# First up-projection chunk: a place of its own for the last row block, reordered transfers, some weight sums on GpSimd, and gathers listed ahead of the unit's own share

## The chip, the cores and the metric

The kernel runs on one core of a Trainium2 chip. Its time is the device time of one execution in microseconds (us). The engines are PE (TensorE), DVE (VectorE), ACT (ScalarE), POOL (GpSimd) and SP (SyncE, which here only issues transfers). The median of 3 runs before the change is 2326.56 us (2325.76 to 2328.48).

## The reference

One decoder layer over a prompt of 2048 tokens and a sample of 8 x 8 tokens, D_MODEL 1024, D_FF 4096, all in float32:

```python
h = rms_norm(x, g_mix_pre)
# projection, sliding-window attention, gated linear attention
mix = einsum('bte,ed->btd', concat(attn, gla), w_out)
x = x + rms_norm(mix, g_mix_post)

h = rms_norm(x, g_ffn_pre)
u = relu(einsum('btd,df->btf', h, w_up))
f = einsum('btf,fd->btd', u * u, w_down)
x = x + rms_norm(f, g_ffn_post)
```

The change touches the seam between the two halves (the residual of the last row blocks, and the start of the feed-forward part) and the loop over w_down.

## The kernel before

**Products.** Each float32 operand is split into a high and a low fp32r part: ACT copies (high), DVE subtracts (low), and PE multiplies three times (high high, high low, low high); `split_by` and `split_copy` are these two instructions. Both feed-forward products use a scheme of seven products in place of eight on 2 x 2 blocks (Strassen's, in Winograd's form), so that sums of blocks of h, of w_up, of w_down and of the activations are made beforehand. Products are numbered p = 1 to 7; 0, 8 and 9 stand for the sample's part, which is computed plainly.

**Row blocks.** The prompt has 16 blocks of 128 rows (0 to 15), the sample is block 16. `B_ORDER` takes them in the order 0, 4, 1, 5, 2, 6, 3, 7, 16, 8, 12, 9, 13, 10, 14, 11, 15. `residual(i, ...)` is a generator with five yields: (1) squares of the out product on ACT, mean and power (DVE, then POOL's `pow`); (2) scaling by `gpost` into x1; (3) x added, a store of x1 for the end of the layer, square and power again; (4) scaling by `gpre`; (5) eight transposes on PE into PSUM and two ACT copies into `ht`; after that four DVE subtractions and a store of `ht` to `h_d`, for the second block of a pair. `run(res, n)` advances it by n steps. The last block, 15, is advanced step by step inside the first chunk of the up projection.

**Up projection.** `up(g, before)` works on chunk g of 256 columns of w_up: g = 0 to 15 with the first half of the prompt (and the sample), 16 to 31 with the second half. PE runs the products in the order `UP_FIRST` = (1, 0, 2, 8, 5, 7, 9, 6, 3, 4) in chunk 0 and `UP_ORDER` = (1, 5, 7, 0, 6, 3, 8, 2, 9, 4) in the others; after each product, the branch for this p issues what belongs to it. PSUM banks: X (p = 1, 2), Z (5, 3), Y (6), V (7, 4). The tile `s` of a chunk has seven rows of 512; `s[:, 1]` is a copy of X, `s[:, 3]` one of Z. Products p = 3 and p = 2 add to Z and X, so they wait for these copies. `H[p]` is operand p of h: 1 and 2 are made from the transposes, the others are fetched from `h_d` by `fetch_h` and split by `split_h`. Weights: `load_up(g)` fetches the chunk into `raws[g]`, `split_up` splits it, `sums_13` and `sums_24` make the sums (two DVE instructions each), and `split_sums` splits them; the sums of g + 1 are made during chunk g. `load_down` and `sum_down` do the same for w_down, which is stored in `t_d`. At the end of a chunk the generator `end` finishes rows 1 and 2 of `s` in the next chunk, and the tile is stored to `s_d`.

**Places.** `s` of odd chunks lies in pool `st1`, which also holds `ht`; `s` of even chunks in `st0`. Operands 3, 5, 7, 6, 4 and `st0` take the place of w_out's parts, so a transfer into them waits until the last out products have read those. Blocks 11 and 15 get x in the place "h0" of `hs_pool`, one after the other.

**Order.** `te`, `ac`, `dv` and `sy` are `InOrder` wrappers of PE, ACT, DVE and SP: what is issued through them keeps the order of the program. What is issued through `nc.sync`, `nc.vector` or `nc.gpsimd` is put in place by the scheduler. An engine takes its instructions in order, and so does SP: a transfer that waits keeps the later ones waiting.

**Down projection.** 7 passes p (`DOWN_ORDER` = (6, 1, 5, 7, 2, 3, 4)) for each half of the prompt, each of 16 units. A unit n is four banks of three products (`down_products`), with two more into the bank `sam` in passes 1, 5, 2, 3 of the first half. `down_fetch(n + 3)` and `down_split(n + 1)` run ahead. When a pass ends (fc == NFC - 1), its banks are handed as generators to the list `todo`, from which each unit takes work worth 1.4 (`room`): `gather` adds or copies a bank into the result (0.7 each), `gather_sample` reads the sample's bank. The sample's bank exists once, so the next pass that has one writes it only after `gather_sample` has read it.

Of the kernel before, what the change touches and what calls it, by code (L numbers as in the profile page):

```python
# [148 lines left out]
def hybrid_step_kernel(ctx: ExitStack, tc: tile.TileContext, I, O):  # L149
# [1199 lines left out]
    def load_x(i, sync=nc.sync):  # L1349
        last = i in B_ORDER[-2:]  # L1350
# [121 lines left out]

    def sums_13(g):

        (a11, a21), (a12, a22) = quarters(g)
        sums[g] = t = U["t13"].tile([P, KT // 2, 2, P], F32, tag="t", name=f"t13_{g}", bufs=1)
        dv.tensor_tensor(t[:, :, 0], a21, a22, op=ALU.add)
        dv.tensor_tensor(t[:, :, 1], a11, a21, op=ALU.subtract)

    def sums_24(g):  # L1480
# [3 lines left out]
        dv.tensor_tensor(t[:, :, 0], t[:, :, 0], a11, op=ALU.subtract)  # L1484
        dv.tensor_tensor(t[:, :, 1], a12, t[:, :, 0], op=ALU.subtract)
# [15 lines left out]
    res = residual(*early.pop(0))  # L1501
# [23 lines left out]
    run(res)  # L1525
    res_11 = residual(*early.pop(0), ac, dv, te, sy)
    run(res_11, 4)
    res_x[B_ORDER[-1]] = load_x(B_ORDER[-1], sy)[0]
    fetch_h(0, 6)
    load_up(1)  # L1530
    fetch_h(0, 3)
    fetch_h(0, 4)
    split_h(5)
    split_h(7)
    split_sums(0, 24)
# [41 lines left out]
    def up(g, before):  # L1577
# [5 lines left out]
        s = U[f"st{g % 2}"].tile([P, 7, BT], F32, tag="st", name=f"st_{g}", bufs=1)  # L1583
# [3 lines left out]
        for p in UP_FIRST if first else UP_ORDER:  # L1587
# [13 lines left out]
            if p == 1:  # L1601
# [6 lines left out]
                ac.activation(s[:, 1], X, AF.Copy)  # L1608
                if more and not first:
                    sums_13(g + 1)  # L1610
# [5 lines left out]
            elif p == 5:  # L1616
                ac.activation(s[:, 3], Z, AF.Copy)
                if first:
                    split_h(3)
            elif p == 7:  # L1620
                dv.tensor_tensor(s[:, 3], s[:, 3], V, op=ALU.add)
                if first:
# [18 lines left out]
            elif p == 3:  # L1641
# [4 lines left out]
                if first:  # L1646
                    split_up(1, 0)
                    run(res, 1)
# [5 lines left out]
            elif p == 2:  # L1654
                squared(s[:, 0], X)
                if first:
                    run(res, 1)
# [7 lines left out]
        if first:  # L1665
            load_up(2)
# [3 lines left out]
            run(res)  # L1670
# [208 lines left out]
    for n, (sb, p, fc) in enumerate(units):  # L1879
# [31 lines left out]
        del parts[n]  # L1911
        room = 1.4
# [9 lines left out]
        if fc == NFC - 1:  # L1922
            todo.extend(gather(sb, p, j, f, p_) for j, p_ in enumerate(banks))
            if sam is not None:
                todo.append(gather_sample(p, f, sam))
                if p == 5:
                    smp = load_sample(1)
            if p == 3 and sb == 0:
                slow.append(finish(NB, f[NB]))
            if p == 3 or (p == late and sb == 0):  # L1930
                slow.extend(finish(i, f[i]) for i in range(sb * 8 + 4 * (p == late), sb * 8 + 4 * (p == late) + 4))
# [41 lines left out]
```

## Time and profile before

| | us |
|---|---|
| median of 3 runs | 2326.56 |
| the profiled execution | 2328.13 |
| its span | 2326.3 |
| chunk 0 (974.30 to 1012.40) | 38.10 |
| chunk 1 (1012.40 to 1043.54) | 31.14 |
| chunk 2 (1043.54 to 1065.19) | 21.65 |
| chunk 16 (1344.89 to 1372.95) | 28.06 |
| chunk 17 (1372.95 to 1392.27) | 19.32 |

The boundaries are the starts of a chunk's first product in the timeline of PE. In that timeline a line is a run of like instructions: start, length, engine, line of the code, operation, out<-in, shapes and count, and in brackets the idle time before it with what ended it. Line 138 stands for everything that is issued through the `InOrder` wrappers, so there the names of the tiles tell the instructions apart: `uc` is bank Z, `ua` and `ub` are X and Y (the other way round in chunk 0), `ud` and `ue` V; `xnT` the transposes of a row block; `sam` the sample's bank and `both` its copy; `dn` the banks of the down projection, `dsam` its sample's bank, `os` and `ot` its operands; `bx` and `x` the row block in `residual`; `x_d` the store of x1. A line of the waits names who waited, for whom, the sum in us, how often, and the longest.

### The profile page before, as it was taken

The page shows a single profiled execution, that of the slowest core. Times are in us where ns is not written, and L with a number is a line of the kernel's source. Part 1 is how long each engine was busy: PE and PEld are TensorE (multiplying, and loading weights), DVE is VectorE, ACT ScalarE, POOL GpSimd, SP SyncE. Part 2 cuts the span into 40 slices and gives each one's busy share as a digit, 9 for nine tenths or more (in the row PEclk, how much of TensorE's full clock was granted, in tenths as well). Part 3 has the DMA queues.
Part 4 walks back from the last instruction along what each step waited for, and adds up shares of the span by engine and source line. Part 5 has one row for each costly group of instructions (what it writes and reads, how often), then busy time and mean ns, then how long its engine had stood idle before and what let it go on. Part 6 is the DMA issues. An engine that isn't in the chain of part 4 may idle for free.

```text
span 2326.3 us, 34053 instructions
## 1 busy us (share of the span) xinstructions
PE 2227.4 (96%) x11800; PEld 1887.5 (81%) x11800; DVE 1611.7 (69%) x3343; ACT 1210.7 (52%) x2513; POOL 270.9 (12%) x428
## 2 busy tenths in 40 slices
PE   8999999999998899979999999999999999999998
PEld 7888887888887788858888878888887878788886
DVE  5888868877777766666776687777544545755557
ACT  5787755454554444445555565555444434555445
POOL 3566412121211101000000000000000000000000
PEclk9999999999999999989999999999999999999999
DMA  6343231121112445755545566666664755876665
GB/s 228 121 153 121 96 101 64 65 71 51 46 46 91 140 168 184 231 194 203 201 168 183 191 248 223 226 231 220 211 195 150 235 164 172 266 235 219 220 195 199
DMA packets 227266, 391.34 MB, mean 168 GB/s; under 512 B 22945, under 2 KB 134966, under 8 KB 223110
## 3 DMA queue, kind: packets, MB, share of 16 engines
q1 hardware_dynamic: 227094, 389.17, 49.7%
q8 instruction: 93, 1.52, 0.3%
q14 instruction: 79, 0.65, 0.1%
HBM read 254.56 MB, written 135.59 MB: 168 GB/s over the span
## 4 chain that ended last, share of the span: by engine, by line
PE 68%; DVE 17%; ACT 7%; DMA 4%; issue 3%; POOL 1%; SPq 0%; DVEq 0%; POOLq 0%; ACTq 0%
PE dn L138 22%; PE ua L138 7%; PE uc L138 7%; PE out L1237 7%; PE gproj L138 5%; PE ue L138 4%; PE ud L138 4%; PE ub L138 3%; DVE s L138 2%; DMA os<-s_d 2%; PE proj L138 2%; DVE XQ L973 2%; PE sam L138 1%; PE dsam L138 1%; DVE pl L138 1%
## 5 line engine op out<-in xcount | busy, mean ns | idle before, releaser
L138 PE MATMUL dn<-ot,os 128*128 128x512 f32 x2688 | 627.4, 391 | 2.9 <-DVE ot L138 1.9
L138 PEld LDWEIGHTS dn<-ot,os 128*128 128x128 f32 x2688 | 506.6, 189 | 113.7 <-DVE ot L138 5.0
L138 DVE TENSOR_TENSOR os<-os 128x512 fp32r<-128x512 f32 x224 | 154.8, 691 | 249.1 <-ACT os L138 248.5
L138 ACT ACTIVATE os<-os 128x512 fp32r<-128x512 f32 x224 | 141.5, 632 | 294.3 <-DMA os<-s_d 242.5
L138 PE MATMUL gproj<-wg,gx 128*128 128x388 f32 x1408 | 288.9, 352 | 0.4 <-DMA gx<-xt_d 0.4
L138 PEld LDWEIGHTS gproj<-wg,gx 128*128 128x128 f32 x1408 | 246.5, 192 | 13.6 <-issue 13.2
L138 ACT ACTIVATE st<-st 128x512 f32<-128x512 f32 x224 | 141.2, 630 | 141.3 <-DVE st L138 137.2
L138 PE MATMUL uc<-H,s 128*128 128x512 f32 x768 | 187.7, 394 | 8.2 <-ACT st L138 6.6
L138 PE MATMUL ua<-H,w 128*128 128x512 f32 x744 | 179.4, 390 | 0.0
L138 PEld LDWEIGHTS uc<-H,s 128*128 128x128 f32 x768 | 145.6, 190 | 39.9 <-ACT st L138 7.5
L138 PEld LDWEIGHTS ua<-H,w 128*128 128x128 f32 x744 | 139.1, 188 | 28.4
L138 DVE TENSOR_TENSOR st<-st 128x512 f32<-128x512 f32 x160 | 110.7, 692 | 69.4 <-ACT st L138 66.1
L214 POOL TENSOR_TENSOR frs<-rs_v,half 128x1 f32<-128x1 f32 (+1 forms) x13 | 9.2, 704 | 1282.6 <-DVE rs_v L138 1282.6
L1237 PE MATMUL out<-wo,mt 128*128 128x512 f32 x656 | 155.1, 395 | 3.3 <-DVE x L1384 3.3
L1237 PEld LDWEIGHTS out<-wo,mt 128*128 128x128 f32 x656 | 122.2, 188 | 30.8 <-issue 3.5
L138 DVE TENSOR_TENSOR ot<-ot 128x512 fp32r<-128x512 f32 x128 | 88.3, 690 | 23.5 <-ACT ot L138 22.6
L138 ACT ACTIVATE s<-t 128x1024 fp32r<-128x1024 f32 x64 | 67.9, 1060 | 59.3 <-PE ud L138 26.5
L138 PE MATMUL proj<-wa_hi,xh 128*128 128x384 f32 (+1 forms) x272 | 95.9, 356 | 0.6 <-ACT wa_hi L138 0.6
L138 ACT ACTIVATE ot<-ot 128x512 fp32r<-128x512 f32 x128 | 80.8, 631 | 28.9 <-DMA ot<-t_d 25.2
L138 PE MATMUL proj<-wa_lo,xh 128*128 128x384 f32 (+1 forms) x272 | 94.4, 351 | 0.0
L138 PE MATMUL proj<-wa_hi,xl 128*128 128x384 f32 (+1 forms) x272 | 93.3, 347 | 0.0
L138 DVE TENSOR_TENSOR s<-t,s 128x1024 fp32r<-128x1024 f32 x64 | 78.4, 1225 | 20.5 <-ACT s L138 17.4
(363 smaller groups left out, 4073.7 us busy)
## 6 DMA issues: line engine op xcount, KB each, us to landing
os<-s_d SPq DMA_DIRECT2D x224, 256.0 KB, 2.8
s_d<-st SPq DMA_DIRECT2D x31, 1792.0 KB, 8.6
raw<-in_w_up SPq DMA_DIRECT2D x64, 512.0 KB, 4.9
ot<-t_d SPq DMA_DIRECT2D x128, 256.0 KB, 3.8
rt<-in_w_down SPq DMA_DIRECT2D x96, 256.0 KB, 3.0
t<-in_w_down SPq DMA_DIRECT2D x64, 256.0 KB, 3.5
t_d<-t SPq DMA_DIRECT2D x32, 512.0 KB, 7.0
gx<-xt_d SPq DMA_DIRECT2D x28, 512.0 KB, 4.1
```

The costliest lines, as they stand in the source:

```text
L138: ins = call(*a, **k)
L214: nc.gpsimd.tensor_tensor(out, v[:n], e, op=ALU.pow)
L973: nc.vector.tensor_tensor(xq[rr, :, l, r, : n // 2].rearrange("p g (m b) -> p g m b", b=b), dr[rr], qr[rr], op=ALU.mult)
L1237: te.matmul(p_, x, w[:, cc], start=k + u == 0, stop=k == KT - 1 and u == len(products) - 1)
```

## The change

1. `load_x`: block 15 gets x in rows 4 and 5 of chunk 0's tile `s`, which is now allocated early as `s_first`, in place of "h0".
2. Transfers: the fetches of operands 6, 3, 4, the load of x and `load_up(1)` come before block 11's residual, and with it before its store. Block 14's residual issues its stores through `sy`.
3. Chunk 0: `split_h(7)`, `split_sums(0, 24)` and `split_h(3)` move behind products 1, 2 and 7; steps 3, 4 and 5 of block 15 move to p = 5, 7 and 6; its end and its store come before `load_up(2)` and the sums of chunk 1.
4. Chunk 1: ACT's copies of X and Z move behind p = 7.
5. `sums_13` and `sums_24` of chunks 1, 16 and 17 run on GpSimd.
6. Down projection: the list `todo` is filled before the unit takes its share, in the last unit of the pass itself; the sample comes first.

```diff
@@ -1347,7 +1347,10 @@
         nc.sync.dma_start(t, I[name][0].partition_broadcast(P))
 
     def load_x(i, sync=nc.sync):
-        last = i in B_ORDER[-2:]
+        if i == B_ORDER[-1]:
+            x = s_first[:, 4:6].rearrange("p a t -> p (a t)")
+            return x, sync.dma_start(x, x_rows(i))
+        last = i == B_ORDER[-2]
         pool, tag, bufs = (hs_pool, "h0", 1) if last else (R["x"], "x", 2)
         x = pool.tile([P, D], F32, tag=tag, name=f"bx_{i}", bufs=bufs)
         return x, sync.dma_start(x[: rows(i)], x_rows(i))
@@ -1470,19 +1473,22 @@
     def quarters(g):
         return [[raw[:, :, u * P : (u + 1) * P] for u in range(2)] for raw in raws[g]]
 
+    def sums_on(g):
+        return nc.gpsimd if g in (1, NFC, NFC + 1) else dv
+
     def sums_13(g):
 
         (a11, a21), (a12, a22) = quarters(g)
         sums[g] = t = U["t13"].tile([P, KT // 2, 2, P], F32, tag="t", name=f"t13_{g}", bufs=1)
-        dv.tensor_tensor(t[:, :, 0], a21, a22, op=ALU.add)
-        dv.tensor_tensor(t[:, :, 1], a11, a21, op=ALU.subtract)
+        sums_on(g).tensor_tensor(t[:, :, 0], a21, a22, op=ALU.add)
+        sums_on(g).tensor_tensor(t[:, :, 1], a11, a21, op=ALU.subtract)
 
     def sums_24(g):
 
         (a11, a21), (a12, a22) = quarters(g)
         t = sums[g]
-        dv.tensor_tensor(t[:, :, 0], t[:, :, 0], a11, op=ALU.subtract)
-        dv.tensor_tensor(t[:, :, 1], a12, t[:, :, 0], op=ALU.subtract)
+        sums_on(g).tensor_tensor(t[:, :, 0], t[:, :, 0], a11, op=ALU.subtract)
+        sums_on(g).tensor_tensor(t[:, :, 1], a12, t[:, :, 0], op=ALU.subtract)
 
     def split_sums(g, n):
         halves_[g, n] = parts = [
@@ -1498,7 +1504,7 @@
             split_up(0, 0, nc.scalar, nc.vector)
             split_up(0, 1, nc.scalar, nc.vector)
             res_x[B_ORDER[-2]] = load_x(B_ORDER[-2])[0]
-    res = residual(*early.pop(0))
+    res = residual(*early.pop(0), sync=sy)
     run(res, 5)
     close_pools(R)
     open_pools(U, ("sam", "s13h", "t13", "s13l", "s24h"), "u")
@@ -1523,16 +1529,15 @@
     fetch_h(0, 5)
     fetch_h(0, 7)
     run(res)
+    fetch_h(0, 6)
+    s_first = U["st0"].tile([P, 7, BT], F32, tag="st", name="st_0", bufs=1)
+    res_x[B_ORDER[-1]] = load_x(B_ORDER[-1], sy)[0]
+    fetch_h(0, 3)
+    fetch_h(0, 4)
+    load_up(1)
     res_11 = residual(*early.pop(0), ac, dv, te, sy)
     run(res_11, 4)
-    res_x[B_ORDER[-1]] = load_x(B_ORDER[-1], sy)[0]
-    fetch_h(0, 6)
-    load_up(1)
-    fetch_h(0, 3)
-    fetch_h(0, 4)
     split_h(5)
-    split_h(7)
-    split_sums(0, 24)
     fold = cpool.tile([P, NS], F32, name="fold")
     nc.vector.tensor_tensor(fold, ident[:, :NS], ident[:, NS:], op=ALU.add)
     res = residual(B_ORDER[-1], last_banks, ac, dv, te, sy, "ec")
@@ -1580,7 +1585,7 @@
 
 
         sb, fc = divmod(g, NFC)
-        s = U[f"st{g % 2}"].tile([P, 7, BT], F32, tag="st", name=f"st_{g}", bufs=1)
+        s = U[f"st{g % 2}"].tile([P, 7, BT], F32, tag="st", name=f"st_{g}", bufs=1) if g else s_first
         first, more = g == 0, g + 1 < NG
         X, Z, Y, V = (bank([P, BT], kind, f"u{kind}_{g}") for kind in ("ab"[first], "c", "ba"[first], "de"[g % 2]))
         sam = bank([P, BT], "b", f"sam_{fc}") if sb == 0 else None
@@ -1605,8 +1610,11 @@
                 if g + 2 < NG and not first:
                     load_up(g + 2)
                 deque(before, 0)
-                ac.activation(s[:, 1], X, AF.Copy)
-                if more and not first:
+                if g != 1:
+                    ac.activation(s[:, 1], X, AF.Copy)
+                if first:
+                    split_h(7)
+                elif more:
                     sums_13(g + 1)
                 sum_down(g, 1)
                 if not more:
@@ -1614,12 +1622,17 @@
                     down_fetch(1)
                     down_fetch(2)
             elif p == 5:
-                ac.activation(s[:, 3], Z, AF.Copy)
+                if g != 1:
+                    ac.activation(s[:, 3], Z, AF.Copy)
+                if first:
+                    run(res, 1)
+            elif p == 7:
+                if g == 1:
+                    ac.activation(s[:, 1], X, AF.Copy)
+                    ac.activation(s[:, 3], Z, AF.Copy)
+                dv.tensor_tensor(s[:, 3], s[:, 3], V, op=ALU.add)
                 if first:
                     split_h(3)
-            elif p == 7:
-                dv.tensor_tensor(s[:, 3], s[:, 3], V, op=ALU.add)
-                if first:
                     run(res, 1)
                 elif more:
                     split_sums(g + 1, 13)
@@ -1645,7 +1658,6 @@
                 squared(s[:, 6])
                 if first:
                     split_up(1, 0)
-                    run(res, 1)
             elif p == 8 and sb == 0:
                 both = U["sam"].tile([P, FC], F32, tag="sam", name=f"both_{fc}", bufs=1)
                 ac.activation(both, sam[:, :FC], AF.Copy)
@@ -1654,6 +1666,7 @@
             elif p == 2:
                 squared(s[:, 0], X)
                 if first:
+                    split_sums(0, 24)
                     run(res, 1)
             elif p == 9 and sb == 0:
                 for u in range(2):
@@ -1663,11 +1676,11 @@
             if not more and p in (3, 2):
                 down_split(p == 2)
         if first:
+            run(res)
             load_up(2)
             split_sums(1, 13)
             sums_24(1)
             split_sums(1, 24)
-            run(res)
         if g in (0, NFC):
             for k in range(2):
                 load_down(k + (g > 0) * first_sums)
@@ -1909,6 +1922,19 @@
             for u, t in enumerate(parts[n][1]):
                 te.matmul(sam, smp[:, fc], t, start=fc + u == 0, stop=fc == NFC - 1 and u == 1)
         del parts[n]
+        if fc == NFC - 1:
+            if sam is not None:
+                todo.append(gather_sample(p, f, sam))
+            todo.extend(gather(sb, p, j, f, p_) for j, p_ in enumerate(banks))
+            if sam is not None:
+                if p == 5:
+                    smp = load_sample(1)
+            if p == 3 and sb == 0:
+                slow.append(finish(NB, f[NB]))
+            if p == 3 or (p == late and sb == 0):
+                slow.extend(finish(i, f[i]) for i in range(sb * 8 + 4 * (p == late), sb * 8 + 4 * (p == late) + 4))
+            if p == 3 and sb == 1:
+                slow.extend(prepare_last(12 + j, j, f[12 + j]) for j in range(4))
         room = 1.4
         while todo and room > 0:
             cost = next(todo[0], None)
@@ -1919,18 +1945,6 @@
         for _ in range(1 + (sb == 1 and p == late)):
             while slow and not todo and next(slow[0], slow) is slow:
                 slow.popleft()
-        if fc == NFC - 1:
-            todo.extend(gather(sb, p, j, f, p_) for j, p_ in enumerate(banks))
-            if sam is not None:
-                todo.append(gather_sample(p, f, sam))
-                if p == 5:
-                    smp = load_sample(1)
-            if p == 3 and sb == 0:
-                slow.append(finish(NB, f[NB]))
-            if p == 3 or (p == late and sb == 0):
-                slow.extend(finish(i, f[i]) for i in range(sb * 8 + 4 * (p == late), sb * 8 + 4 * (p == late) + 4))
-            if p == 3 and sb == 1:
-                slow.extend(prepare_last(12 + j, j, f[12 + j]) for j in range(4))
     close_pools(Dp)
     close_pools(U)
     hs_pool.release()
```

## The prediction

> **What bounds the kernel now.** The page comes first, then the table by stretches, then PE's waits in each bad stretch, then the timelines.
>
> ```profile
> span 2326.3 us, 34053 instructions
> PE 2227.4 (96%) x11800; PEld 1887.5 (81%) x11800; DVE 1611.7 (69%) x3343; ACT 1210.7 (52%) x2513; POOL 270.9 (12%) x428
> ```
>
> PE is busy 96% of the span, so only stretches where PE waits, or runs at a low clock after waiting, can give time back. The columns below are: stretch, its length, then busy time (instructions) of PE, PEld, DVE, ACT, POOL, granted clock, DMA share, GB/s.
>
> ```profile
> 974.30:1012.40 38.10, 27.00 (x121) 21.82 (x120) 23.78 (x28) 22.20 (x34) 1.62 (x3) 0.87 0.61 210
> 1012.40:1043.54 31.14, 24.75 (x106) 20.00 (x104) 22.96 (x34) 12.72 (x23) 0.00 (x0) 0.89 0.64 214
> 1043.54:1065.19 21.65, 21.65 (x106) 18.29 (x105) 14.87 (x22) 11.46 (x19) 0.00 (x0) 1.00 0.59 202
> 1344.89:1372.95 28.06, 22.45 (x85) 17.38 (x84) 24.68 (x29) 19.37 (x28) 0.00 (x0) 0.89 0.74 266
> 1372.95:1392.27 19.32, 19.32 (x85) 15.96 (x84) 14.91 (x23) 9.54 (x15) 0.00 (x0) 0.99 0.57 204
> 1753.97:1767.07 13.10, 8.98 (x29) 6.88 (x28) 5.26 (x8) 5.47 (x10) 0.00 (x0) 0.74 0.26 81
> 1767.07:1773.44 6.37, 6.37 (x29) 5.26 (x28) 1.34 (x2) 1.88 (x3) 0.00 (x0) 1.00 0.51 165
> 1907.10:1918.00 10.90, 8.26 (x30) 6.32 (x28) 5.73 (x9) 3.79 (x6) 0.00 (x0) 0.84 0.30 98
> ```
>
> Chunks 0, 1 and 2 of the up projection are the first three rows: chunk 2 is PE from end to end; chunks 0 and 1 lose 38.1 + 31.1 - 2 x 21.65 - 1.8 (the transposes of two rows of x, 0.9 each) = 24.1 us. Chunk 16 (fourth row) loses 28.06 - 19.32 = 8.7 against chunk 17. In the down stage two pairs of units take 13.10 and 10.90 where a pair takes 6.37: 6.7 and 4.5 lost. Who is waited for:
>
> ```profile
> PE xnT L138 <- DVE x L138: 8.8, 1, 8.8
> PE uc L138 <- ACT st L138: 5.3, 1, 5.3
> PE sam L138 <- ACT both L138: 1.1, 1, 1.1
> PE ud L138 <- ACT H L138: 3.8, 1, 3.8
> PE dsam L138 <- ACT fs L138: 4.1, 1, 4.1
> PE dsam L138 <- DVE fs L138: 2.6, 1, 2.6
> ```
>
> **The down stage: +10.3 us.** The two dsam waits have one cause. One PSUM bank holds the sample's product; the next pass with a sample (6,1,5,7,2,3,4: after 1 comes 5, after 2 comes 3) may write it only after `gather_sample` has read it. That is listed behind four gathers, two a unit, from one unit later on, so ACT and DVE reach it three units late. The change lists it first, and before the splits of the next unit.
>
> ```profile
> 1760.97 1.22 PE L138 MATMUL dsam<-ot,smp 128*128 128x512 f32 x2 [4.12 <-ACT fs L138]
> 1759.85 1.07 ACT L138 ACTIVATE fs<-dsam 128x512 f32<-128x512 f32 x2
> 1761.99 4.79 PE L138 MATMUL dn<-ot,os 128*128 128x512 f32 x12
> L138 ACT ACTIVATE os<-os 128x512 fp32r<-128x512 f32 x224 | 141.5, 632 | 294.3 <-DMA os<-s_d 242.5 <-PE dn L138 34.4 <-DVE ot L138 6.2
> L138 DVE TENSOR_TENSOR f<-f,dn 128x512 f32<-128x512 f32 x56 | 36.7, 681 | 1.1 <-PE dn L138 0.8
> ```
>
> Pass 1 ends on PE at 1753.97, where the row of 13.10 begins. The two copies (1.07) then end at 1755.1, before the next sample product is due (1753.97 + 2.72 = 1756.7): no wait, and no slow matmuls behind it. The cost: these reads and a gather now stand ahead of the splits of the unit after next, which PE needs at 1757.1. ACT: copies 1755.1, gather's copy 0.5, two splits 1.1: 1756.8; DVE's low part 0.7 later, 1757.5: about 0.2 late, and some 0.4 more as the remaining gathers pass. At 2 to 3 there are only DVE additions (0.68 each), done well within a unit. Of 6.7 + 4.5 = 11.2 I keep 10.3; ends 8 (each pass change loses some 0.25) and 11.2. The other pass changes have the same gathers one unit earlier; the tightest is pass 6, whose four ACT copies (0.5 apart, the last after PE's last product) end 0.6 past the pass; splits then end 2.4 past it and PE needs them at 2.7. Nothing, with 0.3 to spare.
>
> **Chunks 0 and 1: +4.1 us.** What ends last there is a chain through the last row (15). Its parts now:
>
> ```profile
> 980.38 0.33 SPq L138 DMA_DIRECT2D bx<-in_x_prompt  x1
> 980.60 0.59 ACT L138 ACTIVATE x<-out 128x512 f32<-128x512 f32 x1
> 992.13 1.06 ACT L138 ACTIVATE H<-H 128x1024 fp32r<-128x1024 f32 x1 [2.71 <-DMA H<-h_d]
> 996.24 1.22 DVE L138 TENSOR_TENSOR bx<-x,bx 128x1024 f32<-128x1024 f32 x1
> 1004.73 1.28 DVE L138 SCALAR_TENSOR_TENSOR x<-bx,ssq,gpre 128x1024 f32<-128x1024 f32 x1
> 1006.15 1.94 PE L138 MATMUL xnT<-ident,x 128*128 128x128 f32 x8 [8.81 <-DVE x L138]
> 1006.08 2.43 SPq L138 DMA_DIRECT2D raw<-in_w_up  x2
> 1016.97 2.74 DVE L138 TENSOR_TENSOR ht<-ht 128x512 f32<-128x512 f32 x4
> 1019.77 0.52 SPq L138 DMA_DIRECT2D h_d<-ht  x1
> 1028.57 0.60 ACT L138 ACTIVATE st<-ua 128x512 f32<-128x512 f32 x1 [4.67 <-DMA h_d<-ht]
> 1030.70 1.34 DVE L138 TENSOR_TENSOR t<-t 128x256 f32<-128x256 f32 x3 [0.38 <-DMA t<-in_w_down]
> 1039.80 0.37 ACT L138 ACTIVATE both<-sam 128x256 f32<-128x256 f32 x1
> 973.00:976.00 3.00, 3.00 (x15) 2.45 (x14) 1.06 (x3) 2.63 (x4) 0.54 (x1) 1.00 1.15 349
> L138 DVE TENSOR_TENSOR H<-H,H 128x1024 fp32r<-128x1024 f32 x22 | 25.9, 1221 | 11.2 <-ACT H L138 11.1
> ```
>
> Transfers: now x and operands 6, 3, 4 stand on SP behind row 11's store and start at 980.4. Without it they start as PE's last out products free their places: 6 from about 971.6, x at 974.3, then 3, 4 and chunk 1's weights. At 349 GB/s, with 2 MB ahead of them, they land near 980.5, 982, 985, 988 and 991. Row 15's chain below needs the first four at 984.6, 989, 991.5 and 998: hidden by its own work, and each us beyond that would move the chain by as much. Row 11's store, behind them all, has no hurried reader. x has a place of its own in chunk 0's tile (rows 4 and 5, written again only when the chunk ends, after 1010), so it waits for no store. Row 14's stores only join SP's written order, in which they stand today already: nothing.
>
> Row 15's end, in the new order of ACT and DVE (a 1024-wide step is 0.95 apart on ACT, 1.14 on DVE, back to back; 512-wide half). Operand 7 goes behind chunk 0's first product and is there by 981.2, PE needs it at 985.3: nothing. ACT squares the row from 980.5, as now, to 982.1; s0 983.3; sums 24 984.3; `both`; operand 6 986.5. DVE: sums 24 to 985.5, the row's scaling 986.8, operand 6 989.1, and then x's addition from 989.1 (now 996.24) to 990.3. ACT squares it to 991.5 and splits operand 3 to 993.4; the power on POOL (0.5) lies beside that. DVE: operand 3 from 992.5 to 994.8, the last scaling to 996.1, 10 us before now. PE runs free to the end of p=6, at 991.1. The transposes are now issued with p=6, ahead of p=3, so PE waits 5 us there, and operand 4 and p=3 behind it: the wait has moved and shrunk, not gone. From the transposes to the store of h: 1.6, p=3 at the low clock 4.8 (as the 12 behind 1761.99), s6 0.7, two squares 1.2, one split (ACT then DVE) 2.2, four subtractions 2.6: 13.1 us, now 13.6.
>
> GpSimd. The sums of chunk 1 leave DVE (4 x 0.68) for POOL (4 x 1.3). The row below shows what POOL does to DVE:
>
> ```profile
> 773.41 1.27 POOL L945 TENSOR_TENSOR sg<-sg,ggla 128x512 f32<-128x512 f32 x1
> 773.51 1.32 DVE L969 TENSOR_TENSOR XK<-dec,qk 128x128 f32<-128x128 f32 x1
> L969 DVE TENSOR_TENSOR XK<-dec,qk 128x128 f32<-128x128 f32 x96 | 27.7, 304 | 0.9
> L138 DVE TENSOR_TENSOR t<-raw,raw 128x512 f32<-128x512 f32 x32 | 21.9, 684 | 2.7 <-PE xnT L1407 2.7
> ```
>
> A DVE operation of 0.30 with both inputs in SBUF took 1.32 beside POOL's and ended with it. So each sum can hold DVE for 1.3. Chunk 1's first two may run once its weights are there (991), just when DVE splits operand 3: between 0 (DVE first) and 2.6. I take 1.7. [...]
>
> Behind the store. Chunk 2's weights (1 MB) and four pieces of w_down now queue behind it on SP, the weights moved past it. Today w_down's second piece lands 10.9 after the store's issue (1019.77 to 1030.7); with 1 MB more at 349 GB/s 13.7. DVE waits for it in order, and from there to the end of the sample's copy (`both`, 1040.17) it is 9.5, unchanged. The two copies that now wait for the store (4.67) stand later on ACT and no longer hold p=3; but PE, ready for the sample's fold about 5 us before `both`, waits there instead, and p=4 behind it runs slow (1.9). So: 996.1 + 1.7 + 13.1 + 13.7 + 9.5 + 3.4 (`both` to chunk 2, 1040.17 to 1043.54) + 1.9 = 1039.4 for chunk 2's start, now 1043.54: 4.1. Also queued: sums 24 of chunk 1 on POOL hold ACT and DVE some 2.6 while PE has slack. Ends: 10.5 (no hold 1.7, no later landing 2.8, no slow clock 1.9) and -1 (held 2.6; the power behind the sums on POOL, 1.6 more; landing 2.6 later).
>
> **Chunks 15 and 16: -1.5 us.** Eight sums go to POOL. DVE is what holds PE in chunk 16 (24.68 of 28.06). Two sums (1.2) leave the path to the last wait (ud); in return POOL can hold DVE 1.3 each time at operand 1 in chunk 15, which stands ahead of `both`, and PE is waiting for that already, and at s3 ahead of `ud`.
>
> ```profile
> 1341.59 0.66 PE L138 MATMUL sam<-fold,both 128*128 128x64 f32 x4 [0.20 <-ACT both L138]
> ```
>
> Ends +1.2 (no hold) and -5.8 (two holds at each place, with 0.7 of slow clock in chunk 15). I take -1.5, nearer to no hold: the first two sums of each chunk can run early, beside an idle DVE, and only the second two meet it.
>
> **Sum.** 10.3 + 4.1 - 1.5 = 12.9. The profiled execution took 2328.13 (span 2326.3 and 1.8 around): 2315.2. It lies 1.6 above the median of 2326.56, so the median comes to 2313.7.
>
> **Rivals.** About 0.2% (4.7 us) is what a measurement of this kernel can tell.
> - DVE is first, POOL holds nothing: 5.8 + 1.2 + 10.3 = 17.3, 2309.3. For it: POOL needs its inputs late. Against: the row at 773.51. Chance 0.20.
> - The weights of chunk 2 don't delay w_down and the fold's wait goes: 10.3 + 10.5 - 1.5 = 19.3, 2307.3. Against: SP's order. 0.12.
> - Sums stand ahead of row 15's power on POOL and hold operand 3 too, PE stays as late as now: 10.3 - 1 - 3 = 6.3, 2320.3. 0.13.
> - It doesn't do what it says: ACT reaches the sample's copies late all the same, as it waits for operands 242.5 us in all. 4.1 - 1.5 = 2.6, 2324.0. 0.07.
> - Slower: the gathers, waiting for PE's last products in DVE's and ACT's order, make the splits behind them late at all 13 pass changes. It eats up the forecast's 12.9 from 1.0 each on, is measurably slower from 1.35, and at 2.0 each costs 26: 2339.7. Against: 0.3 to 2 us in hand at each. 0.05.
> - The forecast: 0.43.
>
> **How the numbers follow.** Terms at their ends give 23 to 1 saved, 2303.6 to 2325; with the last two cases left out (0.12) and the outer tails, 2304 to 2322. Faster by over 0.2% (below 2321.9): the forecast, the first two rivals and most of the third, 0.83; within: 0.12; slower: 0.05.
>
> **What would show it.** Right: no dsam wait over 0.5; the transposes of row 15 near 998 after a PE wait of 5 to 7; the store of h near 1011; a wait at the sample's fold of chunk 1 in place of that at `uc`; DVE operations over 1.2 beside POOL's in chunks 0, 15 and 16. Wrong: x or operand 3 landing after 992; DVE lines of usual length beside POOL; PE waits on `os` or `ot` at each pass.

## The result, and the profile after

| | before | after |
|---|---|---|
| first timing, median of 6 runs each, us | 2326.16 (2324.28 to 2328.48) | 2319.70 (2316.60 to 2320.04) |
| ratio after to before, 95% interval | | 0.9969 [0.9956, 0.9982] |
| second timing, 14 and 9 runs, us | 2328.00 | 2320.36 |
| its ratio | | 0.9967 [0.9956, 0.9978] |
| profiled execution, us (its span) | 2328.13 (2326.3) | 2319.51 (2317.7) |

The kernel became faster by 0.3%: 6.5 us in one timing, 7.6 in the other. The forecast was 12.9 (2313.7); the time lies in its range, which was wide (2304 to 2322). The sign is right, and half of the size is missing. The time falls on the figure of the third rival (2320.3), but by chance: the sums on POOL did not stand ahead of row 15's power, as that rival has it.

The stretches of the changed kernel by the profile's windows; columns as in the prediction (stretch, its length, PE, PEld, DVE, ACT, POOL, granted clock, DMA share, GB/s). The rows are chunks 0, 1, 2, 15 and 16.

```profile
976.21:1008.62 32.41, 25.49 (x121) 21.11 (x120) 22.86 (x25) 20.98 (x34) 5.06 (x5) 0.89 0.62 215
1008.62:1041.69 33.07, 25.23 (x105) 19.83 (x105) 23.21 (x33) 13.72 (x24) 2.57 (x2) 0.90 0.76 248
1041.69:1063.20 21.51, 21.51 (x105) 18.13 (x104) 14.64 (x21) 11.30 (x19) 0.00 (x0) 1.00 0.50 181
1321.12:1347.94 26.82, 24.58 (x105) 20.23 (x104) 18.35 (x18) 16.82 (x23) 7.32 (x4) 0.88 0.92 346
1347.94:1372.97 25.03, 21.47 (x85) 17.02 (x84) 20.27 (x24) 16.37 (x25) 3.27 (x2) 0.92 0.67 227
```

Chunks 0 and 1 together take 65.48 (69.24 before); chunks 15 and 16 51.85 (50.00: chunk 15 ran from 1322.95 to 1344.89, and chunk 16 took 28.06). From chunk 17's start to the end of the span it is 944.73 (2326.3 - 1372.95 = 953.35 before). Chunk 0 itself began at 976.21, not 974.30: that is 1.9 us lost ahead of chunk 0. Chunk 2 before ends at 1065.03, where chunk 3's first product starts, and not at 1065.19 as in the table before; it took 21.49, so it has not changed (21.51). So 3.8 - 1.85 + 8.6 - 1.9 = 8.65, the difference of the two spans (8.6).

Who PE waits for, from chunk 0 on (who, for whom: us in total, times, longest):

```profile
PE sam L138 <- ACT both L138: 7.5, 2, 5.3
PE xnT L138 <- DVE x L138: 6.5, 1, 6.5
PE dn L138 <- DVE f L138: 2.9, 1, 2.9
PE ud L138 <- ACT H L138: 2.8, 1, 2.8
PE uc L138 <- ACT st L138: 1.2, 1, 1.2
```

Both `dsam` rows are gone. The wait at `uc` has shrunk from 5.3 to 1.2, and a wait for `both` at the sample's fold (the product `sam<-fold,both`) has taken its place, as the prediction said. New and not forecast is the third row: PE waits 2.9 us for DVE's addition into `f`. PE's timeline (start, length, operation, tiles, count, and in brackets the wait before it) shows these places:

```profile
999.85 1.94 PE L138 MATMUL xnT<-ident,x 128*128 128x128 f32 x8 [6.50 <-DVE x L138]
1035.92 1.12 PE L138 MATMUL sam<-fold,both 128*128 128x64 f32 x4 [5.31 <-ACT both L138]
1036.80 5.05 PE L138 MATMUL ue<-H,w 128*128 128x512 f32 x12
1760.60 2.80 PE L138 MATMUL dn<-ot,os 128*128 128x512 f32 x11 [0.20 <-DVE ot L138]
1951.05 2.20 PE L138 MATMUL dn<-ot,os 128*128 128x512 f32 x9
1956.14 12.04 PE L138 MATMUL dn<-ot,os 128*128 128x512 f32 x45 [2.88 <-DVE f L138]
```

The first three are the path through row 15 (block 15). Twelve such products take 2.88 at a granted clock of 1.00 (chunk 2); the 12 behind the fold's wait took 5.05. Products that take longer than that are called slow below. The fourth is the first pass change with a sample: 0.2 us late, which is the 0.2 of the prediction. The last two are the end of pass 3: the next unit gets through three of its four banks (9 of 12 products) and stops at 1953.25, since the fourth bank has not been read out. What DVE does meanwhile:

```profile
1951.25 0.69 DVE L138 TENSOR_TENSOR fs<-fs,dsam 128x512 f32<-128x512 f32 x1 [4.78 <-PE dsam L138]
1953.06 1.22 DVE L138 TENSOR_TENSOR fs<-fs,fs_fold 64x1024 f32<-64x1024 f32 x1 [1.12 <-ACT fs_fold L138]
1954.20 0.68 DVE L138 TENSOR_TENSOR os<-os 128x512 fp32r<-128x512 f32 x1
1954.81 0.68 DVE L138 TENSOR_TENSOR ot<-ot 128x512 fp32r<-128x512 f32 x1
1955.41 1.27 DVE L138 TENSOR_TENSOR f<-f,dn 128x512 f32<-128x512 f32 x2
```

In pass 3 the sample's step does not end with its first addition: it also folds the sample's result (a copy on ACT, then a DVE addition that waits for it). Listed first, it waits for the sample's last product, then goes to ACT and back, and only behind two splits comes the first gather, at 1955.41, which sets PE free.

GpSimd's sums in chunk 0 and beside operand 1 in chunk 15, first POOL's timeline (its first row is the power of row 15), then DVE's:

```profile
993.45 0.54 POOL L214 TENSOR_TENSOR ssq<-rs_v,half 128x1 f32<-128x1 f32 x1 [8.62 <-DVE rs_v L138]
993.96 1.27 POOL L1484 TENSOR_TENSOR t<-raw 128x512 f32<-128x512 f32 x1
995.18 2.25 POOL L1483 TENSOR_TENSOR t<-raw,raw 128x512 f32<-128x512 f32 x1
1331.72 1.67 POOL L1490 TENSOR_TENSOR t<-t,raw 128x512 f32<-128x512 f32 x1 [12.20 <-DVE s L138]
1333.46 2.15 POOL L1491 TENSOR_TENSOR t<-raw,t 128x512 f32<-128x512 f32 x1
```

```profile
994.10 4.41 DVE L138 TENSOR_TENSOR H<-H,H 128x1024 fp32r<-128x1024 f32 x2 [0.20 <-ACT H L138]
1332.16 4.54 DVE L138 TENSOR_TENSOR H<-hraw,H 128x1024 fp32r<-128x1024 f32 x2
```

A pair of low parts takes 2.36 when it is alone (e3 below); here 4.41 and 4.54. Later, in chunk 1, ACT waits for POOL's second pair of sums:

```profile
1016.38 1.06 ACT L138 ACTIVATE s<-t 128x1024 fp32r<-128x1024 f32 x1 [6.86 <-POOL t L1491]
```

### The profile page after: what moved, and what is told of

It is laid out like the page before. It is cut to its first block, busy times and chain, and to the rows that moved or that the text cites. A ratio compares the mean times of both kernels' runs of the same rounds, so it can differ in the third digit from the quotient of the medians.

```text
span 2317.7 us, 34065 instructions
## 1 busy us (share of the span) xinstructions
PE 2224.0 (96%) x11800; PEld 1885.6 (81%) x11800; DVE 1609.6 (69%) x3331; ACT 1210.2 (52%) x2513; POOL 290.1 (13%) x440
## 4 chain that ended last, share of the span: by engine, by line
PE 71%; DVE 16%; ACT 6%; issue 3%; DMA 2%; POOL 1%; DVEq 0%; SPq 0%; ACTq 0%; POOLq 0%
PE dn L138 25%; PE uc L138 7%; PE ua L138 7%; PE out L1237 7%; PE gproj L138 5%; PE ue L138 4%; PE ud L138 4%; PE ub L138 3%; DVE s L138 2%; PE proj L138 2%; DVE XQ L973 2%; PE sam L138 1%; PE dsam L138 1%; DVE pl L138 1%; PE gm L138 1%
## 5 line engine op out<-in xcount | busy, mean ns | idle before, releaser
L138 PE MATMUL dn<-ot,os 128*128 128x512 f32 x2688 | 625.0, 390 | 5.0 <-DVE f L138 2.9
```

The lines of the kernel that those rows point to most:

```text
L138: ins = call(*a, **k)
```

## The experiments

Three stretches are compared throughout; boundaries are starts of a chunk's first product in PE's timeline, the last one runs to the end of the span. "Time" is the median, or the one execution where no interval stands (e5 to e8). A ratio is to the kernel before as timed along with that run, and these times differ: 2327.86 for e1 to e4, 2328.00 for e9 to e12; the one execution beside e5 to e8 took 2327.96.

| kernel | chunks 0 + 1 | 15 + 16 | 17 to end | time | ratio to before |
|---|---|---|---|---|---|
| before | 69.24 | 50.00 | 953.35 | 2326.16 | |
| after | 65.48 | 51.85 | 944.73 | 2319.70 | 0.9969 [0.9956, 0.9982] |
| e1 down stage only | 68.24 | 49.80 | 944.82 | 2320.89 | 0.9967 [0.9951, 0.9982] |
| e2 all but the down stage | 66.38 | 51.97 | 947.91 | 2324.31 | 0.9986 [0.9972, 1.0] |
| e3 all sums on DVE | 65.31 | 49.24 | 947.79 | 2314.86 | 0.9945 [0.9927, 0.9964] |
| e4 sample last at pass 3 | 65.29 | 51.86 | 941.62 | 2313.97 | 0.994 [0.9922, 0.9958] |
| e5 chunk 2's weights earlier | 63.57 | 52.50 | 946.14 | 2318.99 | |
| e6 old transfers | 65.51 | 51.72 | 944.40 | 2314.74 | |
| e7 transfers only | 65.61 | 49.99 | 949.86 | 2320.99 | |
| e8 copies of X, Z back | 65.27 | 51.96 | 945.26 | 2317.58 | |
| e9 after, again | 65.60 | 51.85 | 945.32 | 2320.36 | 0.9967 [0.9956, 0.9978] |
| e10 `both` ahead | 62.71 | 52.05 | 947.87 | 2314.38 | 0.9936 [0.9922, 0.9949] |
| e11 three edits | 62.09 | 50.00 | 942.35 | 2309.56 | 0.9917 [0.9902, 0.9932] |
| e12 four edits | 59.00 | 50.00 | 943.22 | 2306.44 | 0.9904 [0.9889, 0.992] |

How to read it: where the code of the stretch is the same, the first column differs by up to 1.1 us (68.24 and 69.24 in e1 and before; 65.29 to 66.38 in after, e2, e4 and e9) and the second by up to 0.8, so differences of 2 and more in them carry the verdicts on the seam. The third scatters by some 3, and the start of chunk 0 lay anywhere from 971.95 (e6) to 978.39 (e2) although no experiment changed anything much earlier. A single time of a kernel (e5 to e8) is therefore no verdict.

**e1 and e2: the two halves of the change.** e1 is the kernel before with part 6 alone (the list filled in the last unit, the sample first); e2 is everything else.

> The kernel before with the change to the list of the down projection alone. Theory (the two sample waits go, a new wait of 2.9 us with slow matmuls behind it, 4.6 in all, comes where pass 3 ends): the stretch from the first unit that waits (1753.97 in the profile of before) to the end loses 6.3 + 4.5 - 4.6 and some 1.8 in the last pass, 8 to 9 us; ratio to before 0.9965, about 2318. Rival (the down stage runs faster only because the up stage before it changed what is in flight): less than 4 us. In either case chunks 0 and 1 keep 69.2 us and chunks 15 and 16 keep 50.0.

> The whole change without the part on the list of the down projection. Theory: chunks 0 and 1 take 65.5 us as in the profile of after (69.2 before), chunks 15 and 16 51.9 (50.0 before), the down stage as before with both sample waits (4.1 and 2.6): 1.9 us in all, ratio 0.999, not to be told from no change. Rival (the up part carries the gain and the down part little): 4 us or more, ratio under 0.9983.

e1 has no `dsam` wait, and the new wait of 2.88 at the end of pass 3, here in its PE timeline:

```profile
1958.94 16.40 PE L138 MATMUL dn<-ot,os 128*128 128x512 f32 x64 [2.88 <-DVE f L138]
```

e2 has both `dsam` waits and not this one. So both come from part 6. In time e1 came as expected: 0.9967, and 8.53 us less from chunk 17 on than before. e2 is less clear: it is 3.6 us below the kernel before timed with it, where 1.9 was expected, and its ratio (0.9986, interval to 1.0) lies between the theory and the rival, so the time does not decide between them. Chunks 0 and 1 missed the expected figures by 1.0 and 0.9 (68.24 and 66.38), without any difference in their code. By the medians the whole change (0.9969) is no faster than part 6 alone; what the seam gives on top, some 1 us by the first two columns, is less than these timings can tell.

e2 also shows something that the waits alone do not. PE's timeline in the kernel before, then in e2, at the same two places:

```profile
1760.97 1.22 PE L138 MATMUL dsam<-ot,smp 128*128 128x512 f32 x2 [4.12 <-ACT fs L138]
1761.99 4.79 PE L138 MATMUL dn<-ot,os 128*128 128x512 f32 x12
...
1912.63 1.12 PE L138 MATMUL dsam<-ot,smp 128*128 128x512 f32 x2 [2.64 <-DVE fs L138]
1913.54 4.16 PE L138 MATMUL dn<-ot,os 128*128 128x512 f32 x12
```

```profile
1762.89 0.73 PE L138 MATMUL dsam<-ot,smp 128*128 128x512 f32 x2 [3.13 <-ACT fs L138]
1763.46 2.91 PE L138 MATMUL dn<-ot,os 128*128 128x512 f32 x12
...
1912.29 0.73 PE L138 MATMUL dsam<-ot,smp 128*128 128x512 f32 x2 [2.71 <-DVE fs L138]
1912.86 2.89 PE L138 MATMUL dn<-ot,os 128*128 128x512 f32 x12
```

A wait of 2.64 was followed by slow products in one execution (4.16 for 12), a wait of 2.71 at the same place by products at full speed in the other (2.89). The granted clock over these 12 products was 0.57 and 0.67 in the kernel before (first and second place); in e2 they took 2.91 and 2.89, where 12 take 2.88 at a clock of 1.00 (chunk 2). e7, which also has the old list, had one of each: 3.89 behind a wait of 3.34, 2.90 behind one of 2.97.

**e3: no sums on GpSimd.**

```diff
-        return nc.gpsimd if g in (1, NFC, NFC + 1) else dv
+        return dv
```

> The whole change with all weight sums on DVE again. Theory (a sum on POOL holds DVE's two-input operations, and hands its result on later): chunks 15 and 16 back to 50.0 us from 51.9; in chunk 0 the split of operand 3 takes 2.4 us on DVE and not 4.4, so the transposes of row 15 stand 2 us earlier, and ACT's wait of 6.9 for POOL's sums goes, against 2.4 us more work on DVE: chunks 0 and 1 take 62 to 64 us, not 65.5. In all about 4 us faster than the whole change, 2315 to 2316. Rival (POOL takes work off a DVE that is the bound): chunks 0 and 1 take 67 to 68, chunks 15 and 16 52 or more; slower than the whole change by 2 to 4.

DVE's timeline (operand 3's low parts, then the first sum of chunk 2), and PE's at the transposes:

```profile
993.14 2.36 DVE L138 TENSOR_TENSOR H<-H,H 128x1024 fp32r<-128x1024 f32 x2 [0.20 <-ACT H L138]
1023.23 0.69 DVE L138 TENSOR_TENSOR t<-raw,raw 128x512 f32<-128x512 f32 x1 [2.65 <-DMA raw<-in_w_up]
```

```profile
996.84 1.94 PE L138 MATMUL xnT<-ident,x 128*128 128x128 f32 x8 [4.46 <-DVE x L138]
```

Operand 3 takes 2.36 for 4.41, and the transposes begin 996.84 - 975.24 = 21.60 after chunk 0's start (999.85 - 976.21 = 23.64 in the changed kernel): the hold is real and costs 2.04 there. Chunks 15 and 16 come back to 49.24, and the median is 4.8 to 5.5 below that of the changed kernel's two timings. But chunks 0 and 1 gain next to nothing (65.31, where 62 to 64 was expected): DVE now waits 2.65 for chunk 2's weights. These are issued on SP behind the store of h, and their landing is what comes late next; e11 below, which has both edits, bears it out.

**e4: the sample behind the gathers at pass 3 alone.**

```diff
-            if sam is not None:
+            if sam is not None and p != 3:
                 todo.append(gather_sample(p, f, sam))
             todo.extend(gather(sb, p, j, f, p_) for j, p_ in enumerate(banks))
+            if sam is not None and p == 3:
+                todo.append(gather_sample(p, f, sam))
```

> The whole change, but where pass 3 ends the sample's step stands behind the four gathers again. Theory (the sample's fold takes 2.0 of a share of 1.4, so the first gather comes a unit late, and PE's fourth bank of pass 4 waits for it): the wait of 2.9 us goes and the slow matmuls with it, 4 to 5 us faster than the whole change, about 2315. Rival (any gather ahead of the splits makes PE wait there): a wait of 1 us or more stays at the start of pass 4, and the time stays above 2318.

PE's timeline at the end of pass 3, then DVE's:

```profile
1948.29 0.62 PE L138 MATMUL dsam<-ot,smp 128*128 128x512 f32 x2
1948.74 19.43 PE L138 MATMUL dn<-ot,os 128*128 128x512 f32 x85
```

```profile
1946.44 1.37 DVE L138 TENSOR_TENSOR f<-f,dn 128x512 f32<-128x512 f32 x2 [2.31 <-PE dn L138]
1948.93 1.28 DVE L138 TENSOR_TENSOR f<-f,dn 128x512 f32<-128x512 f32 x2
```

The first gathers run ahead of the sample's last product, and PE goes through without a stop. The median is 5.7 to 6.4 below that of the changed kernel's two timings, of which this stretch explains 3.4: from chunk 17 to the end the kernels with the sample last (e4, e11, e12) average 942.4, those with the change's order (after, e1, e3, e5, e6, e8, e9, e10) 945.8, and those with the old code (before, e2, e7) 950.4.

**e5: chunk 2's weights ahead of row 15's end.**

```diff
         if first:
-            run(res)
             load_up(2)
+            run(res)
```

> The changed kernel with one move: chunk 2's weights are issued on SP ahead of the last row's end and of its store of h, no longer behind them. Measure: chunks 0 and 1 together, from the first product of chunk 0 to that of chunk 2 (69.24 us before, 65.48 after). Theory (weights behind the store are what the sums of w_down and the sample's copy of chunk 1 wait for at the end): DVE's wait for them (1.13 after, 2.65 with all sums on DVE) goes, 64.4 us, or 64.0 if the slow matmuls at the sample's fold shrink with it. Rival (the chain through the store of h and the squares decides, the weights are hidden): 65.5. A second rival: the store now stands behind 1 MB and lands 3 us later, and ACT's copies of X and Z of chunk 1, which need its place, wait: over 66.5.

Chunks 0 and 1 get another 1.9 us shorter (63.57); 64.0 to 64.4 was expected, and the difference is within the scatter. DVE no longer waits for the weights, and PE's wait at the fold is shorter, with p=4 behind it less slow:

```profile
1034.23 1.11 PE L138 MATMUL sam<-fold,both 128*128 128x64 f32 x4 [4.07 <-ACT both L138]
1035.10 4.20 PE L138 MATMUL ue<-H,w 128*128 128x512 f32 x12
```

The second rival (the store late behind 1 MB) did not show: the store of h is issued 36.5 after chunk 0's start (36.3 in the changed kernel), and ACT's copies of X and Z, at 1022.3, wait for nothing.

**e6 and e7: steps without transfers, transfers without steps.** e6 is the changed kernel with the old order on SP and the old place of x; e7 is the kernel before with the new ones (row 14's stores go through `sy` in both):

```diff
+    fetch_h(0, 6)
+    s_first = U["st0"].tile([P, 7, BT], F32, tag="st", name="st_0", bufs=1)
+    res_x[B_ORDER[-1]] = load_x(B_ORDER[-1], sy)[0]
+    fetch_h(0, 3)
+    fetch_h(0, 4)
+    load_up(1)
     res_11 = residual(*early.pop(0), ac, dv, te, sy)
     run(res_11, 4)
-    res_x[B_ORDER[-1]] = load_x(B_ORDER[-1], sy)[0]
...
```

> The changed kernel with the old order of transfers and the old place of x for row 15: the fetches of operands 6, 3 and 4, x and chunk 1's weights stand behind row 11's store again; the steps of row 15, the sums on GpSimd and the down stage stay as changed. Measure: chunks 0 and 1 together (65.48 after), and when row 15's transposes begin, counted from chunk 0's start (23.64 after, 31.85 before). Theory (the steps carry the gain, the transfers only have to be there by then): operand 6 lands 11.3 and 13.5 after chunk 0's start as before, operand 3 17.8 and 19.1; row 15's addition moves by 1.1, the transposes begin between 22.5 and 25; 65 to 67 us. Rival (the transfers carry it): the transposes at 28 or later, 68 us or more.

> The kernel before with the transfers alone: the new order on SP and x of row 15 in chunk 0's tile; row 15's steps, all sums and the down stage stay as before. Measure: chunks 0 and 1 together (69.24 before, 65.48 after), and the transposes of row 15 from chunk 0's start (31.85 before). Theory (in the kernel before ACT waited 1.3, 1.1 and 2.7 us for operands 6 and 3, and row 15's addition stood behind their low parts on DVE, so half of the gain is in the transfers): the addition comes 3 to 5 us earlier, the transposes at 27 to 29; 65.5 to 67 us. Rival (only the steps carry it): 68.5 to 69.3. The prediction's own order of things (transfers in time only hidden by the steps' move) has no gain from transfers alone: it is the rival.

In one profile each, either half alone brings chunks 0 and 1 to where the whole change has them. The windows of e6, then of e7 (chunks 0 and 1):

```profile
971.95:1004.58 32.63, 25.32 (x122) 20.86 (x120) 21.99 (x25) 21.20 (x34) 5.59 (x5) 0.90 0.61 213
1004.58:1037.46 32.88, 24.88 (x105) 19.59 (x105) 23.21 (x33) 13.72 (x24) 2.58 (x2) 0.90 0.75 248
```

```profile
974.30:1006.69 32.39, 25.87 (x121) 21.51 (x120) 23.23 (x27) 21.77 (x34) 1.62 (x3) 0.89 0.73 247
1006.69:1039.91 33.22, 25.81 (x105) 20.72 (x104) 23.48 (x34) 12.83 (x24) 0.00 (x0) 0.85 0.63 210
```

The paths differ. In e6 the transposes begin 995.81 - 971.95 = 23.86 after chunk 0's start (23.64 in the changed kernel): ACT waits 0.96 and 1.41 for operand 6 in the old order, and that costs at most 0.2 there. PE and DVE in e7:

```profile
1000.96 1.94 PE L138 MATMUL xnT<-ident,x 128*128 128x128 f32 x8 [5.76 <-DVE x L138]
1024.52 5.18 PE L138 MATMUL uc<-H,s 128*128 128x512 f32 x12 [5.80 <-ACT st L138]
1025.51 1.34 DVE L138 TENSOR_TENSOR t<-t 128x256 f32<-128x256 f32 x3 [0.39 <-DMA t<-in_w_down]
```

In e7 the transposes begin at 1000.96 - 974.30 = 26.66 (31.85 before), since ACT no longer waits for operands 6 and 3; and the store of h is issued 40.28 after chunk 0's start, 4 us later than the 36.33 of the changed kernel. Yet chunk 2 starts at the same distance. In e7 the weights of chunk 2 stand ahead of that store, as before the change, and only w_down's pieces behind it: 10.93 from the store to the second piece (1025.51) and 9.46 to the end of `both`. In the changed kernel the weights stand behind the store too, and the two parts are 12.2 and 11.1. So what is queued behind the store and DVE's work on it take 3 of the 4 us back, and the two halves together give no more than one. That this order on SP is the whole reason is argued from these two chains; e5 tests it for the changed kernel, where it is worth 1.9.

**e8: copies of X and Z of chunk 1 back behind p=1 and p=5.**

> The changed kernel with ACT's copies of X and Z of chunk 1 back behind p=1 and p=5, where they wait for the store of h to land. Measure: chunks 0 and 1 together (65.48 after). Theory (the store now lands some 8 us after its issue at 1012.5, before or about when ACT comes to the copies): within 0.5 of 65.5. Rival (the later place is what keeps PE from waiting): a wait of 3 us or more at uc of chunk 1, as the 5.3 before, and 67 us or more.

65.27, with the wait at `uc` at 1.23 as in the changed kernel: ACT comes to these copies late in either place, without waiting for the store, and their move did nothing.

**e9 to e12: what stands together.** In e10 `both` goes ahead on ACT in chunk 1:

```diff
-                if more and not first:
+                if more and g > 1:
                     split_sums(g + 1, 24)
-                squared(s[:, 6])
+                if g != 1:
+                    squared(s[:, 6])
...
                 ac.activation(both, sam[:, :FC], AF.Copy)
+                if g == 1:
+                    split_sums(2, 24)
+                    squared(s[:, 6])
```

e11 is e3, e4 and e5 in one kernel; e12 is e11 and e10.

> The changed kernel once more, on the same chip as the next three, so that they can be compared with it and not only with the kernel before. Expected: 2319 to 2320 us, ratio to before 0.996 to 0.998, as in its first timing (0.9969); chunks 0 and 1 65.5, chunks 15 and 16 together 51.9, the wait of 2.9 at the end of pass 3.

> The changed kernel with one edit: in chunk 1, ACT's copy of the sample's bank (both) is issued ahead of the splitting of chunk 2's sums 24 and of the squares of row 6 of s, which in the changed kernel stand before it on ACT and wait for DVE. Theory (PE's 5.3 at the sample's fold is ACT's order: the bank is full 6 us before ACT comes to it, held by instructions that wait for a late DVE): the wait falls below 1, p=4 behind it runs at full clock (2.9 for 5.05), chunks 0 and 1 together 65.5 - 5.3 - 2.1 + what comes late next in chunk 2: 59 to 62. Rival (DVE's work is the bound, the wait only moves into chunk 2): 59 to 62 for the two chunks, but chunk 2 takes 4 to 7 us more than its 21.65 and the whole is as after. Ratio to before: 0.9945 by the theory, 0.997 by the rival.

> The changed kernel with three edits of the earlier runs together: the sample's step behind the gathers at pass 3, all weight sums on DVE, chunk 2's weights ahead of the store of h. By the terms of the single runs (3.9 from pass 3, 2.6 from chunks 15 and 16, 1.9 to 3 from chunks 0 and 1, since the landing of chunk 2's weights was what held the run with all sums on DVE): 8 to 9 us below the changed kernel, ratio to before 0.9925 to 0.9935. If the edits hide one another (the time that DVE takes for the sums in chunk 0 delays the store as far as the weights' earlier landing helps): chunks 0 and 1 stay at 63.5 to 65 and 6 us remain.

> The kernel of the run before this one (three edits) and the copy of the sample's bank ahead in chunk 1. Theory as for the single edit: 4 to 6 us below the run before it, chunks 0 and 1 together 57 to 60, chunk 2 at 21.7, ratio to before 0.9905 to 0.9915. Rival (DVE's work in chunk 1 is the bound): chunk 2 longer by what chunk 1 gains, same time as the run before it.

e9 repeats the first timing: 2320.36, ratio 0.9967, 65.60 and 51.85, and a wait of 2.89 at the end of pass 3.

e10: less than half of the 7.4 us (5.3 + 2.1) came. The wait at the fold fell to 2.97 (not below 1), p=4 behind it was still slow (4.59), and chunks 0 and 1 gained 2.9 against e9; the median, 6.0 below e9, fell by more than that explains. Chunk 2 took 1060.26 - 1038.71 = 21.55, so nothing moved into it: the rival is out. What still holds `both` is a square that waits for DVE, in ACT's timeline of e10:

```profile
1032.20 1.29 ACT L138 ACTIVATE st<-st 128x512 f32<-128x512 f32 x2 [3.83 <-DVE st L138]
1033.40 0.37 ACT L138 ACTIVATE both<-sam 128x256 f32<-128x256 f32 x1
```

DVE is busy from 1024.97, when the weights land, until that square: here the order on ACT and the work on DVE each have a part.

e11 was better than expected (10.8 us below e9): chunks 0 and 1 reach 62.09, so the sums on DVE and the earlier weights help each other (3.4 together, 0.2 and 1.9 alone), as the 2.65 of e3 says. e12 is 3.1 below e11, less than the 4 to 6 expected and with overlapping intervals; in the profiles chunks 0 and 1 fall by the same 3.1, to the 59.00 that was expected (57 to 60). It beats the changed kernel by 13.9 us and the kernel before by 0.96% [0.8, 1.11].

## Why the prediction was right, and where it was wrong

**The down stage (+10.3; measured 8.6 in the profiled pair, 4.6 on average).** The mechanism holds for the two waits: both go, and the first pass change is late by the 0.2 that was worked out. Two things were wrong in the sum.
- The step that failed is "The other pass changes have the same gathers one unit earlier; the tightest is pass 6 [...] Nothing, with 0.3 to spare." The list was checked for what comes before the sample's step, not for what that step holds at pass 3: a fold over ACT and back to DVE, ahead of the gather that frees PE's next bank. It cost a wait of 2.88 and 1.84 of slow products (12.04 for 45, which at 2.72 for 12, back to back, are 10.2). The wait is 2.9 in all eight profiles with this order; the slow products behind it come in five of them (last section). With the step behind the gathers, e4 has no wait there and the time comes back.
- A size was off: of the 11.2 lost before, 2.5 + 1.8 were slow products behind the waits (1.22 + 4.79 and 1.12 + 4.16, against 0.62 + 2.88 each). That part is not there in every execution: in e2 both places ran at full speed. One profile gave its own draw, and the sum took it as fixed. On average the old code had 950.4 - 942.4 = 8 to lose there, by three profiles on each side.

**Chunks 0 and 1 (+4.1; measured 3.8 in the profiled pair).** Between the averages of the same code (before and e1; after, e2, e4 and e9) it is 3.05, so the closeness of 3.8 is in part luck. The path is right but for two links. Counted from chunk 0's start: the transposes at 23.6 (forecast 997.8 - 974.3 = 23.5), the store of h at 36.3 (36.6), PE's wait at the fold 5.3 (5), p=4 slow by 2.2 (1.9), chunk 2 at 65.5 (65.1). The first wrong link carries another name: it is not w_down's second piece that DVE waits for but chunk 2's weights, ahead of it on SP. The changed kernel's SP and DVE rows:

```profile
1012.54 0.53 SPq L138 DMA_DIRECT2D h_d<-ht  x1
1013.16 5.98 SPq L138 DMA_DIRECT2D raw<-in_w_up  x2
```

```profile
1024.73 0.69 DVE L138 TENSOR_TENSOR t<-raw,raw 128x512 f32<-128x512 f32 x1 [1.13 <-DMA raw<-in_w_up]
```

12.2 from the store to this sum, then 11.2 until `both` is done and PE starts on the fold (1035.92): 23.4 where the prediction had 13.7 + 9.5 = 23.2. The sum is right and its two parts are not. What it said of SP's order ("the weights moved past it") is borne out by e5, in one profile: with the weights ahead of the store the two chunks take 1.9 less. In the changed kernel SP waited 20.2 for DVE's `ht` before it issued the store, and the weights behind it followed at 1013.16; in e7, ahead of the store, they were issued from 993.21 on. The second wrong link is the later place of the copies of X and Z, which was to free p=3: e8 shows that it does nothing; the wait at `uc` shrank as the store is issued 3.9 after chunk 1's start (7.4 before). What the prediction did not see is that either half of the change would do (e6, e7).

**GpSimd.** The hold of 1.7 was 2.04. It meets operand 3 and not the power, which stands ahead of the sums on POOL (993.45 and 993.96): the third rival is out. So is the one without a hold, and the one in which the fold's wait goes (it is 5.31). The hold shows on both engines: DVE's pair beside POOL took 4.41 for 2.36, and POOL's second sum 2.25, where the first took 1.27 and those of chunk 1, beside an idle DVE, 1.29 and 1.28. The hold by sums 24 of chunk 1 was put at 2.6 while PE has slack; ACT waited 6.86 for them, and then DVE 3.86 for ACT (2.74 and 1.13 in the kernel before). It cost little only while DVE had to wait for chunk 2's weights anyway: with these earlier, taking all sums off POOL gave 1.5 more (63.57 in e5, 62.09 in e11, one profile each).

**Chunks 15 and 16 (-1.5; measured -1.85).** The kernels with the sums on POOL there (after, e2, e4, e5, e6, e8, e9, e10) take 51.7 to 52.5, and e1, e3, e7, e11 and e12 without them 49.2 to 50.0. Where the holds fall varies (chunk 15 took 26.82 in the changed kernel, 23.99 in e5, with chunk 16 the other way round); the sum hardly does.

**The rival that was slower** (splits late at all 13 pass changes) did not happen: from 1740 on, PE's waits for `ot` from DVE sum to 1.6 (1.7 before). One pass change is late, for another reason. **The start of chunk 0**, 1.9 us later, lies within its scatter: with the same code up to there it was 974.30 in before and 978.23 in e1. What moves it stays open.

## What to carry to other kernels

When a step is moved to the head of a list, price everything it holds at each place where the list is used, round trips between engines too, and ask what behind it sets another engine free. Two edits that each shorten a path need not add up, when a later step takes back what one of them gains: try each alone, and look for what is queued behind the store that was moved ahead. A stall's price read from one profile has a fixed part, the wait, and a part that differs from execution to execution, the slow products behind it (0.3 to 3.2 us here behind the same wait of 2.9); count the second only in part.

## What the runs showed of the hardware

- Slow products behind a short wait come and go. At the same two places, waits of 2.6 to 4.1 us were followed by 12 products in 4.79 and 4.16 (before), 2.91 and 2.89 (e2). At the end of pass 3 the wait was 2.9 in eight profiles. What came behind it up to 1980, by PE's timeline in six of them: 109 products in 25.00 (e9), 98 in 24.06 (after), 86 in 21.39 (e1), 100 in 24.57 (e5), 102 in 26.32 (e10) and 107 in 27.31 (e3); the granted clock over the first 6 us was 0.73 in after. Against 2.72 for 12 that is a loss of 0.3 in e9, 1.8 or 1.9 in after, e1 and e5, and 3.2 and 3.1 in e10 and e3 (an estimate). In e6 and e8, for which all 2688 `dn` products stand together, they were busy for 624.0 and 624.4, against 623.7 in e4, without the wait, and 625.0 in after: little was lost there. The two with the largest loss have the longest third column of the eight (947.79 and 947.87).
- In chunk 0 a pair on DVE that overlapped two sums on POOL took 4.41 (2.36 in e3, without them), and the second sum 2.25 (1.27 the first): moving DVE's work to POOL beside a busy DVE cost more than it saved (chunks 15 and 16: 51.85 against 49.24 with the sums on DVE alone, e3).
- The same code up to there (after, e2, e4, e5, e8, e9, e10) reached chunk 0 at times 4.5 us apart (973.87 to 978.39). That is more than half of the whole gain.
